# The second MLP of a two-layer block in two phases, with seven half products on each side

## The chip, the cores and the metric

The kernel runs on one NeuronCore of one Trainium2 chip. The metric is the device time of one execution in microseconds (us). Five engines work beside each other and meet through semaphores: TensorE (PE, matrix products), VectorE (DVE), ScalarE (ACT), GpSimd (POOL) and SyncE (SP, which issues most transfers). 16 DMA engines move data between DRAM and the core.

## The reference, cut to what matters

```python
for i in range(2):                      # layer 0: pooling mixer, layer 1: attention
    sh1, sc1, gt1, sh2, sc2, gt2 = ada_mods(c, w_ada[i], b_ada[i])
    ...                                 # the mixer of the layer
    m_lat = sq_relu_mlp(modulate(rms_norm(x, g_mlp_pre[i]), sh2, sc2), w_mlp_in[i], w_mlp_out[i])
    x = x + gt2 * rms_norm(m_lat, g_mlp_post[i])

def sq_relu_mlp(h, w_in, w_out):
    return jnp.square(jax.nn.relu(h @ w_in)) @ w_out
```

All of it is f32. The model width is 1024 and the hidden width of an MLP is 4096. The first MLP runs on 512 latent and 256 context tokens, the second on the 512 latent tokens alone. The second MLP therefore is a product of 512x1024 by 1024x4096 (the in-product), a squared relu, and a product of 512x4096 by 4096x1024 (the out-product).

## The kernel before, in words

**Precision.** Each f32 operand is split into a high part (a rounded copy, made by a cast on ACT) and a low part (the operand less its high part, a subtraction on DVE). A product of two f32 blocks is three matmuls: high by high, high by low, low by high. A "split" below means this pair of instructions.

**Groups and pairs.** The hidden width is cut into 16 groups of 256 columns; groups 2p and 2p+1 are pair p. Each group has 1 MB of in-weights and 1 MB of out-weights.

**The first MLP** (functions `mlp0`, `weights_sums`, `Seven`, `Halves`) has two phases. In the in-phase, groups 2 to 15 are done by `Seven`: the 2x2 block product of a group is formed from seven half products instead of eight, at the price of sums of weight blocks and sums of row blocks (`sums`, made once). The squares of a pair, and four sums of them, go to DRAM as seven row blocks (`lefts`, 384 KB each, written through POOL's queue). In the out-phase, `Halves` runs over the pairs in passes: pass by pass it takes one or two of the seven out-products, loads weights and row blocks again, splits them, and sums all seven pairs in the same PSUM banks, so that no product is added in SBUF until its last pair. Weights are loaded five steps ahead and prepared three steps ahead. An intermediate sum of weights (`halfway`) is written to DRAM in one pass and read back in a later one.

**The second MLP** (`mlp1`, lines 1210 to 1364) runs in one phase over seven pairs. Per pair it makes the in-products of two groups directly (`Inner`, L657: 48 matmuls of 128x512 for each group; the first two groups in column chunks of 256, 96 matmuls each), relus (L668) and squares (L1258) on ACT, and then the seven out-products of the pair before (`product`, L1267: two token tiles of six 128x512 matmuls each, 84 in all). Each half of a product is added to an accumulator in SBUF by DVE (L1271; the first pair is copied by ACT). Weight splits are at L1234 (out-weights and rows, with the sums at L1240) and at L199 and L202 (in-weights). Groups 14 and 15 are left for `finish`, which multiplies them by their out-weights directly, adds the accumulators and normalises.

**Buffers.** Working tiles of 128x1024 come from a ring of three (`work_tile`), raw weights of 1 MB from another ring of three (`rawp`). PSUM has eight banks: four in the pool `psB`, and either two double ones or four single ones in `psA` (`sum_banks`).

**What sets the order.** Up to the second MLP's first pair a scheduler places the instructions by its own estimate of their times; between `pin(True)` and `pin(False)` (in the first MLP) each engine's instructions stand in the order in which the program issues them. On every engine, and on every DMA issue queue, an instruction that waits holds up those behind it.

## Time and profile before

| | |
|---|---|
| time, median of 3 runs | 1119.65 us (1119.57 to 1119.93) |
| the profiled execution's own time | 1120.31 us |
| its span in the trace | 1118.5 us, so 1.8 us lie around the span |
| PE, DVE, ACT, POOL busy | 1099.2, 922.4, 620.2, 108.7 us |
| first MLP: in-phase, out-phase | up to 314 us, 314 to 514 us (49 steps of 18 matmuls) |
| second MLP | from about 783 us; the pairs to about 1089; the end to 1118 us |

The profile gives, for each engine, busy time and groups of equal instructions (line, engine, operation, output and inputs by the program's names, shape, count, busy time and mean time of one). Matmuls overlap, so the busy time of one (0.39 us for 128x512) is longer than the step from one start to the next. L95 is the line of a helper through which all instructions of the pinned parts go; they are told apart by the names of their tiles. `PEclk` is the granted clock of TensorE as a share of full speed.

### The profile page before, as it was taken

What the parts mean: (1) busy time and instruction counts of PE and PEld (TensorE: products, weight loads), DVE (VectorE), ACT (ScalarE), POOL (GpSimd) and SP (SyncE); (2) the same over time, 40 slices, a digit from 0 to 9 for tenths busy, and PEclk for the clock granted to TensorE, in tenths of its full rate; (3) what the DMA queues carried; (4) which work ended last, traced back from release to release, by engine and by line L of the source; (5) the groups of instructions that cost most, each with busy time, mean ns of one, the idle gap of its engine ahead of it and who ended that gap; (6) DMA issues with size and microseconds to landing.
All of it is one profiled execution on the core that took longest, in us unless ns stands there. A gap on an engine that the chain in (4) does not pass through costs nothing. (4 is left out here: it accounts for less than half of the span.)

```text
span 1118.5 us, 15827 instructions
## 1 busy us (share of the span) xinstructions
PE 1099.2 (98%) x6034; PEld 962.6 (86%) x6034; DVE 922.4 (82%) x1300; ACT 620.2 (55%) x1036; POOL 108.7 (10%) x176
## 2 busy tenths in 40 slices
PE   6999999999999999999999999999999999999997
PEld 6679999999988888887888899989988888888886
DVE  4888989999888889977776699885788888987876
ACT  6686566555564544443764478634674544543622
POOL 1240111111100000001242100002000000000001
PEclk9999999999999999999999999999999999999999
DMA  9984757767689989975211101172343333431212
GB/s 374 419 350 91 288 179 249 249 234 266 237 302 377 360 331 395 376 261 206 80 54 55 38 35 46 37 280 97 140 160 114 122 145 129 160 118 71 113 55 96
DMA packets 53371, 214.97 MB, mean 192 GB/s; under 512 B 7504, under 2 KB 10400, under 8 KB 38704
## 3 DMA queue, kind: packets, MB, share of 16 engines
q1 hardware_dynamic: 46688, 187.36, 45.3%
q0 software_dynamic: 6608, 26.61, 7.0%
q8 instruction: 47, 0.77, 0.3%
q14 instruction: 28, 0.23, 0.1%
HBM read 179.99 MB, written 33.96 MB: 191 GB/s over the span
## 5 line engine op out<-in xcount | busy, mean ns | idle before, releaser
L95 PE MATMUL pso<-ra,sums 128*128 128x512 f32 x594 | 135.8, 389 | 0.0
L95 PEld LDWEIGHTS pso<-ra,sums 128*128 128x128 f32 x594 | 111.5, 188 | 23.2
L657 PE MATMUL psin<-ra,rb 128*128 128x512 f32 (+1 forms) x310 | 87.5, 360 | 0.0
L1267 PE MATMUL pso<-units,pairs 128*128 128x512 f32 x336 | 82.8, 389 | 0.0
L657 PE MATMUL psin<-ra 128*128 128x512 f32 (+1 forms) x256 | 76.6, 376 | 0.0
L1267 PEld LDWEIGHTS pso<-units,pairs 128*128 128x128 f32 x336 | 63.1, 188 | 13.1
L1271 DVE TENSOR_TENSOR acc<-acc,pso 128x512 f32<-128x512 f32 x72 | 48.7, 680 | 22.4 <-PE pso L1267 22.4
L243 POOL TENSOR_SCALAR ms<-ss 128x1 f32<-128x1 f32 x15 | 10.1, 676 | 571.8 <-ACT junk L230 556.1
L95 PE MATMUL psin<-ra,units 128*128 128x384 f32 x340 | 63.4, 334 | 0.0
L657 PEld LDWEIGHTS psin<-ra,rb 128*128 128x128 f32 x310 | 55.5, 189 | 8.7
L95 PE MATMUL psin<-sums,units 128*128 128x384 f32 x308 | 62.4, 334 | 0.0
L95 DVE CUSTOM_DVE_ANT_0 waste<-raw,crow 128x1024 f32<-128x1024 f32 x50 | 61.1, 1222 | 1.3
L95 ACT CAST ra<-work 128x1024 fp32r<-128x1024 f32 x34 | 35.7, 1050 | 45.9 <-DVE work L95 42.4
L95 PEld LDWEIGHTS psin<-ra,units 128*128 128x128 f32 x340 | 59.3, 188 | 0.0
L95 PE MATMUL pso<-ra,rb 128*128 128x512 f32 x252 | 58.3, 389 | 0.0
L657 PE MATMUL psin<-rb,rb 128*128 128x512 f32 (+1 forms) x155 | 55.7, 360 | 0.1
L95 PEld LDWEIGHTS pso<-ra,rb 128*128 128x128 f32 x252 | 47.3, 188 | 9.8
L657 PEld LDWEIGHTS psin<-ra 128*128 128x128 f32 x256 | 47.1, 188 | 8.7
L95 PEld LDWEIGHTS psin<-sums,units 128*128 128x128 f32 x308 | 54.2, 188 | 0.1
L1418 PE MATMUL psq<-units,ra 128*128 128x512 f32 x216 | 52.2, 393 | 0.0
L95 DVE TENSOR_TENSOR ra<-work,ra 128x1024 fp32r<-128x1024 f32 x34 | 41.7, 1225 | 8.8 <-ACT ra L95 8.6
L657 PE MATMUL psin<-rb,ra 128*128 128x512 f32 (+1 forms) x128 | 48.1, 376 | 0.0
(333 smaller groups left out, 2673.5 us busy)
## 6 DMA issues: line engine op xcount, KB each, us to landing
raw<-in_w_ada SPq DMA_DIRECT2D x48, 1024.0 KB, 8.8
raw<-in_w_mlp_in SPq DMA_DIRECT2D x32, 1024.0 KB, 5.5
lefts<-acc POOLq DMA_DIRECT2D x48, 384.0 KB, 4.1
raw<-in_w_mlp_out SPq DMA_DIRECT2D x18, 1024.0 KB, 5.2
wide<-lefts SPq DMA_DIRECT2D x38, 384.0 KB, 7.3
wide<-in_w_mlp_out SPq DMA_DIRECT2D x21, 512.0 KB, 6.8
halfway<-work POOLq DMA_DIRECT2D x14, 512.0 KB, 7.8
raw<-in_w_mlp_out SPq DMA_DIRECT2D x14, 512.0 KB, 7.4
```

Source lines behind the costliest of these rows:

```text
L95: return lambda *args, **kw: self.tc.keep_in_program_order(f(*args, **kw))
L243: gp.tensor_scalar(out=ms[:, 0:1], in0=ss[:, parts - 1:parts], scalar1=rest, scalar2=EPS, op0=ALU.add, op1=ALU.add)
L657: te.matmul(ps[:, bank, o:o + ln], w[:, k, fs], rhs, start=start, stop=(k == KT - 1 and n == 2), skip_group_check=len(ks) < KT or self.paired)
L1267: te.matmul(ps, a, w, start=(m == 0), stop=(m == len(seq) - 1))
L1271: ve.tensor_tensor(out=M[n][:, t], in0=M[n][:, t], in1=ps, op=ALU.add)
L1418: te.matmul(ps, a[:, k, sl], w[:, k % 4, :], start=(k == 0 and n == 0), stop=(k == KT - 1 and n == 2))
```

## The change

The second MLP gets the two phases of the first.

In the ramp, groups 0 and 1 are done as before, and DVE and ACT make four sums of row blocks and their splits (`summed`) and the weights of group 2 (`weights`). Groups 2 to 15 then run through `Seven` with halves of 256 columns: seven products of twelve 128x256 matmuls a group, and two more "fresh" matmuls for each of the groups 2 and 3. Squares and their sums go to `lefts` in seven row blocks of 256 KB a pair. The dots of the last conditioning gate on DVE (sixteen of 512 columns, which stood beside the out-products) become eight of 1024 columns, two beside each of the groups 5, 7, 9 and 11.

The out-phase is a new class `Rows` with two passes: products 0, 4, 5 and 2 of all seven pairs, then products 6, 3 and 1, 49 steps of twelve 128x512 matmuls. A step's weights are a raw block (products 0, 2 and 1) or a difference that DVE makes first (4, 5, 6 and 3). For product 1 the low part is not made by DVE: ACT writes the negated high part and a DMA from POOL's queue adds the weights to it in SBUF. The results of a product are taken out of PSUM once, with its last pair. `xr`, `gate` and `junk` come back from DRAM in the second pass (`back`).

Three places show how the instructions move. DVE in the ramp, from the split of the second group on (`raw` is loaded weights, `work` a working tile, `units`, `ra` and `sums` hold split operands, `acc` rows). Before:

```order
L1234 TENSOR_TENSOR ra<-raw,ra 128x8x128
L1234 TENSOR_TENSOR ra<-raw,ra 128x1024
L1240 TENSOR_TENSOR work<-raw 128x1024
L1234 TENSOR_TENSOR ra<-work,ra 128x1024
L1234 TENSOR_TENSOR units<-raw,units 128x1024
L202 TENSOR_TENSOR rb<-raw,rb 128x2048
```

and now:

```order
L1443 TENSOR_TENSOR ra<-raw,ra 128x8x128
L1386 TENSOR_TENSOR work<-raw 128x1024
L1392 TENSOR_TENSOR work<-raw,work 128x512
L1411 TENSOR_TENSOR work<-acc 128x1024
L1393 TENSOR_TENSOR work<-raw,work 128x512
L1373 TENSOR_TENSOR units<-work,units 128x1024
L1414 TENSOR_TENSOR sums<-work,sums 128x1024
L1411 TENSOR_TENSOR work<-work,acc 128x1024
L1379 TENSOR_TENSOR units<-work,units 128x1024
```

After the split of group 1's weights DVE no longer splits out-weights: it forms sums of weights and of rows in working tiles (L1386, L1392, L1393, L1411) and their low parts (L1373, L1379, L1414). The second working tile that L1392 writes is the first tile of the ring of three come round again.

ACT at the same place now, from the cast of group 1's weights to the copy that stands after the first half product of group 2 (`psin` is PSUM):

```order
L1442 CAST ra<-raw 128x8x128
L668 ACTIVATE work<-psin 128x512 x2
L1439 ACTIVATE acc<-work 128x512 x2
L1372 CAST units<-work 128x1024
L1413 CAST sums<-work 128x1024
L1378 CAST units<-work 128x1024
L1413 CAST sums<-work 128x1024 x3
```

and right behind these rows come `L668` x2, `L1439` x2 for group 1 and then the copy within PSUM of group 2. The relus and squares of group 1 stand behind all casts of sums, where before relus, squares and casts alternated.

POOL's queue now, from the squares of the last pair to the second pass (before, POOL issues nothing in this MLP's pairs):

```order
L95 DMA lefts<-acc 128x2x256 x3
L95 DMA lefts<-acc 128x512 x4
L95 DMA halfway<-work 128x1024 x7
L95 DMA ra<-in_w_mlp_out 128x2x512
L95 DMA rb<-in_w_mlp_out 128x2x512
```

The seven writes of `halfway` belong to the first pass; the reads of weights into the operand slots in `ra` and `rb`, seven in all, are the accumulating transfers for product 1 in the second pass.

The diff, cut to its core:

```diff
@@ -794,7 +794,8 @@
 
         def run(self, behind):
             pool, tag = ((psB, "b"), (psA, "s"))[self.pool]
-            b, a, c, e = (pool.tile([P, 512], F32, tag=tag, name="psin")[:, 0:HN] for _ in range(4))
+            hn = self.to.shape[-1] // 2
+            b, a, c, e = (pool.tile([P, 512], F32, tag=tag, name="psin")[:, 0:hn] for _ in range(4))
...
+    class Rows:
+        PASSES = ((0, 4, 5, 2), (6, 3, 1))
+
...
+            self.rings = [ra[:, 2048 * n:2048 * n + 2048] for n in range(4)] + self.right[:2], \
+                [unit[0][:, 1024 * n:1024 * n + 1024] for n in range(4)] + self.left[:2]
+            self.hiddens, self.raws, self.rows, self.ops, self.banks, self.parts = hiddens, {}, {}, {}, {}, []
...
+        def load(self, j):
+            ps, p, n = self.todo[j]
+            at = lambda u, h: two(w_mlp_out[1, 2 * p + u])[:, :, 512 * h:512 * h + 512]
+            if n in (0, 5, 6, 3):
...
+            self.rows[j] = two(acc[:, c:c + 512])
+            sy.dma_start(self.rows[j], two(lefts[:, p, n, 0:LAT]))
+
+        def prepare(self, j):
+            ps, p, n = self.todo[j]
+            w = self.raws.pop((ps, p, {0: "11", 2: "22", 1: "21"}[n])) if n in (0, 2, 1) else two(work_tile())
+            sub = lambda a, b: ve.tensor_tensor(out=w, in0=a, in1=b, op=ALU.subtract)
+            if n == 0:
+                self.raws[ps, p, "11"] = w
+            if n == 4:
+                sub(self.raws.pop((ps, p, "12")), self.raws.pop((ps, p, "11")))
+                self.raws[ps, p, "t1"] = w
+            elif n == 5:
+                sub(self.raws[ps, p, "22"], self.raws.pop((ps, p, "t1")))
+                gp.dma_start(two(halfway[:, 1, p]), w)
+            elif n == 6:
+                sub(self.raws.pop((ps, p, "22")), self.raws.pop((ps, p, "12")))
+            elif n == 3:
+                sub(self.raws.pop((ps, p, "t2")), self.raws[ps, p, "21"])
+            r, l = (z[j] if j < 4 else g[(j - 4) % 6] for z, g in zip((self.right, self.left), self.rings))
+            wH, wL, aH, aL = two(r[:, 0:1024]), two(r[:, 1024:2048]), two(l[:, 0:512]), two(l[:, 512:1024])
+            a = self.rows.pop(j)
+            sc.copy(aH, a)
+            sc.copy(wH, w)
+            ve.tensor_tensor(out=aL, in0=a, in1=aH, op=ALU.subtract)
+            if n == 1:
+                sc.activation(wL, wH.bitcast(F32), AF.Copy, scale=-1.0)
+                gp.dma_start(wL, two(w_mlp_out[1, 2 * p + 1])[:, :, 0:512], accum_op=ALU.add)
+            else:
+                ve.tensor_tensor(out=wL, in0=w, in1=wH, op=ALU.subtract)
+            self.ops[j] = wH, wL, aH, aL
+
...
+        def multiply(self, j):
+            ps, p, n = self.todo[j]
+            wH, wL, aH, aL = self.ops.pop(j)
+            if p == 0:
+                pool, tag = ((psB, "b"), (psA, "s"))[n in (5, 2, 1)]
+                self.banks[n] = [pool.tile([P, 512], F32, tag=tag, name="pso") for _ in range(2)]
+            for q in range(2):
+                seq = [(a[:, f, P * q:P * q + P], w[:, f, :]) for f in range(2) for a, w in ((aH, wH), (aH, wL), (aL, wH))]
+                for m, (a, w) in enumerate(seq):
+                    te.matmul(self.banks[n][q], a, w, start=(p == 0 and m == 0),
+                              stop=(p == PAIRS - 1 and m == len(seq) - 1), skip_group_check=True)
+                if p == PAIRS - 1:
+                    self.take(n, q, self.banks[n][q])
...
+        def run(self, back):
+            far, last_ = 5, len(self.todo)
+            early = lambda j: j < last_ and self.todo[j][2] == 1
+            self.load(4)
+            self.prepare(2)
+            for j in range(last_):
+                ps, p, n = self.todo[j]
+                if j + far < last_:
+                    self.load(j + far)
+                self.multiply(j)
+                if j + 3 < last_ and not early(j + 3):
+                    self.prepare(j + 3)
+                if early(j + 4):
+                    self.prepare(j + 4)
+                if j in (3, 6):
+                    self.inner_rows(j // 3 - 1)
+                if j == 28:
+                    back()
+                if ps == 1 and 1 <= p <= 4 and n == 3:
...
+            def first_two():
+                w[0] = work_tile()
+                ve.tensor_tensor(out=words(w[0]), in0=rv[:, 1].rearrange("p (m k) n -> p m k n", m=2),
+                                 in1=rv[:, :, 0:4], op=ALU.subtract)
+
+            def last_two():
+                w[1] = work_tile()
+                t2, t4 = (k4(w[1][:, 512 * m:512 * m + 512]) for m in range(2))
+                ve.tensor_tensor(out=t2, in0=b22, in1=k4(w[0][:, 0:512]), op=ALU.subtract)
+                ve.tensor_tensor(out=t4, in0=b21, in1=t2, op=ALU.subtract)
...
+        def summed(n, a, b, op):
+            w = work_tile()
+            ve.tensor_tensor(out=w, in0=a, in1=b, op=op)
+            hi, lo = f[:, 2048 * n:2048 * n + 1024], f[:, 2048 * n + 1024:2048 * n + 2048]
+            sc.copy(hi, w)
+            ve.tensor_tensor(out=lo, in0=w, in1=hi, op=ALU.subtract)
             return w
...
-        def product(n, first_):
-            (aH, aL), (wH, wL) = X[operand[n]], W[n]
-            for t in range(2):
-                ps = psB.tile([P, 512], F32, tag="b", name="pso")
-                seq = [(a[:, f, t * P:t * P + P], w[:, f, :]) for f in range(2) for a, w in ((aH, wH), (aH, wL), (aL, wH))]
-                for m, (a, w) in enumerate(seq):
-                    te.matmul(ps, a, w, start=(m == 0), stop=(m == len(seq) - 1))
-                if first_:
-                    sc.copy(M[n][:, t], ps)
-                else:
-                    ve.tensor_tensor(out=M[n][:, t], in0=M[n][:, t], in1=ps, op=ALU.add)
...
+        def kept(p, n, z):
+            gp.dma_start(two(lefts[:, p, n, 0:LAT]), z)
...
+        def squared(inner, to):
+            for c in range(2):
+                for h in range(2):
+                    if (c, h) not in begun[inner]:
+                        inner.part(c, h)
+            for h in range(2):
+                sc.activation(to[:, h, :], inner.relu(h), AF.Square)
+
...
-        for p in range(NG // 2 - 1):
-            put(W[0], b11, p == 0)
-            put(W[1], both(1024, b22, b12, ALU.subtract, p == 0), p == 0)
-            put(W[2], b21, p == 0)
-            a11, a21 = squares(inner, 0)
...
+        raw = raw_load(w_mlp_in[1, 2])
+        steps, products = weights(2, raw)
+        squared(inner, first_hid)
+        for z in steps:
+            z()
+        w1 = summed(0, a21, a22, ALU.add)
+        w2 = summed(1, w1, a11, ALU.subtract)
+        summed(2, a11, a21, ALU.subtract)
+        summed(3, a12, w2, ALU.subtract)
+        squared(second, odd_hid)
+        raw = raw_load(w_mlp_in[1, 3])
+        sum_banks(True)
+        pin(True)
+        kept(0, 0, first_hid[:, :, 0:hn])
+        due = row_sums(0, first_hid, odd_hid)
+        chain = Rows(hids)
+        squares, late, dots1 = lambda: None, {g: j for j, g in enumerate((5, 7, 9, 11))}, {}
+        for g in range(2, NG):
+            seven = Seven(products, hids[g % 2], g % 2, g < 4)
+            behind = [[] for _ in range(8)]
+            if g < NG - 1:
+                steps, products = weights(g + 1, raw)
+                two_, four, bh, bl, ch, cl, th, tl, uh, ul = steps
+                for n, z in ((0, two_), (0, four), (3, bh), (3, ch), (3, bl), (4, th), (4, cl), (4, tl), (5, uh), (5, ul)):
+                    behind[n].append(z)
...
+            behind[1].append(rows_done)
+            if g in dots1:
+                j, dot = dots1.pop(g)
+                for b, n in enumerate((0, 2)):
+                    behind[n].append(lambda b=b, j=j, dot=dot: ada_dot(1, GT2, j, 1, dot, [accv[:, 3, :]], dot[:, D * b:D * b + D], b))
+            if g % 2 == 0 and g <= 2 * PAIRS:
+                behind[2].append(lambda: [due[n]() for n in range(3)])
+                behind[5].append(lambda: due[3]())
+            if g < NG - 2:
+                raw = raw_load(w_mlp_in[1, g + 2])
+            if g + 1 in late:
+                dots1[g + 1] = late[g + 1], raw_load(w_ada[1, GT2, late[g + 1]])
+            if g == NG - 1:
+                chain.begin()
+                behind[5].append(lambda: chain.prepare(0))
+                behind[7].append(lambda: chain.prepare(1))
+            squares = seven.run(lambda z: [f() for f in behind[z]])
+            if g == 2:
+                sy.dma_start(accv[:, 3, :], silu[0].partition_broadcast(P))
+        squares()
...
-        xr, gate, junk = residents(ctx)
-        for t in range(NL):
-            sy.dma_start(xr[:, t], spill[:, t])
-        finish(1, [(NG - 2 + q, last_[q].hid, wo_[q]) for q in range(2)], range(NL), last, ((5.1, gate_diag, 1, GT2, 0),))
+
+        def back():
+            nonlocal xr, gate, junk
+            xr, gate, junk = residents(ctx)
+            for t in range(NL):
+                sy.dma_start(xr[:, t], spill[:, t])
+
+        chain.run(back)
+        pin(False)
+        finish(1, chain.parts, range(NL), last, ((5.1, gate_diag, 1, GT2, 0),))
 
     alone = [(1, m, j) for m in (GT1, SC2, SH2) for j in range(4)]
```

More of the change, by code (lines that the diff above doesn't have):

```diff
@@ L1288, in mlp1 @@
-        wi = [None, None]
-        hi, lo = (ra[:, z:z + 2048] for z in (0, 2048))
-        hi, lo = (z.rearrange("p (k n) -> p k n", n=256) for z in (hi, lo))
-        put((hi[:, :, P:], lo[:, :, P:]), raw1[0][:, :, P:], True)
+        f = pool.tile([P, 8192], F32R, name="sums")
+        pool.tile([P, 520], F32, name="row")
+        hn = LAT // 2
+        first_hid, odd_hid, even_hid = (two(acc[:, z:z + 1024]) for z in (4096, 5120, 0))
+        hids = [even_hid, odd_hid]
+        mixed_rows = [two(acc[:, z:z + 512]) for z in range(1024, 3072, 512)]
@@ new lines, in kept, with row_sums, one @@
+        def kept(p, n, z):
+            gp.dma_start(two(lefts[:, p, n, 0:LAT]), z)
+        def row_sums(p, even, odd):
+            a11, a21, a12, a22 = (z[:, :, hn * h:hn * h + hn] for z in (even, odd) for h in range(2))
+            s1, s2, s3, s4 = mixed_rows
+            def one(n, d, a, b, op):
+                ve.tensor_tensor(out=d, in0=a, in1=b, op=op)
+                kept(p, n, d)
+            kept(p, 1, a12)
+            kept(p, 3, a22)
+            return [lambda: one(4, s1, a21, a22, ALU.add), lambda: one(5, s2, s1, a11, ALU.subtract),
+                    lambda: one(6, s3, a11, a21, ALU.subtract), lambda: one(2, s4, a12, s2, ALU.subtract)]
@@ new lines, in squared @@
+        def squared(inner, to):
[5 more added lines that the diff above has]
+                sc.activation(to[:, h, :], inner.relu(h), AF.Square)
+        hi, lo = (ra[:, z:z + 2048].rearrange("p (k n) -> p k n", n=256) for z in (0, 2048))
+        for z in (sc.copy(hi[:, :, P:], raw1[0][:, :, P:]),
+                  ve.tensor_tensor(out=lo[:, :, P:], in0=raw1[0][:, :, P:], in1=hi[:, :, P:], op=ALU.subtract)):
+            tc.keep_in_program_order(z)
```

215 lines of the change are left out of this document (98 added, 117 removed).

## The prediction

> **What bounds the kernel now.** I read the page's first part, the costliest groups, then the time line of PE and the table of windows.
>
> ```profile
> PE 1099.2 (98%) x6034; PEld 962.6 (86%) x6034; DVE 922.4 (82%) x1300; ACT 620.2 (55%) x1036; POOL 108.7 (10%) x176
> L1271 DVE TENSOR_TENSOR acc<-acc,pso 128x512 f32<-128x512 f32 x72 | 48.7, 680 | 22.4 <-PE pso L1267 22.4
> ```
>
> PE is busy all the time; DVE's adds of the out-products (L1271, 48.7 us) wait for PE, not PE for them. So the second MLP costs what its matmuls cost. On the time line of PE these rows bracket it (start, duration):
>
> ```profile
> 794.37 0.40 PE L657 MATMUL psin<-ra,rb 128*128 128x256 f32 x2
> 794.61 0.28 PE L657 MATMUL psin<-rb,rb 128*128 128x256 f32 x1
> 803.25 0.40 PE L657 MATMUL psin<-ra,rb 128*128 128x512 f32 x1
> 1088.88 1.52 PE L928 MATMUL pso<-ra,units 128*128 128x512 f32 x6
> ```
>
> From the first 512-column in-product (803.25) to `finish` (1088.88) are 285.63 us. In them stand 14 groups of 48 in-matmuls and 588 out-matmuls, 1260 in all: 226.7 ns each, without a gap. A 256-column matmul takes 120 ns from start to start (two in 0.24 us, at 794.37). In the windows (stretch, then PE, PEld, DVE, ACT and POOL busy, granted clock, DMA share, GB/s) the clock is full:
>
> ```profile
> 184.00:314.00 130.00, 130.00 (x752) 130.00 (x751) 123.93 (x178) 74.70 (x115) 17.76 (x29) 1.00 0.68 245
> 314.00:320.00 6.00, 6.00 (x30) 5.06 (x29) 3.95 (x5) 5.05 (x7) 0.54 (x1) 1.00 1.00 378
> 430.00:480.00 50.00, 50.00 (x222) 41.39 (x221) 45.62 (x47) 24.46 (x28) 0.00 (x0) 1.00 0.97 366
> 844.00:966.00 122.00, 122.00 (x540) 101.02 (x539) 100.54 (x132) 57.88 (x71) 0.00 (x0) 1.00 0.36 130
> ```
>
> The last row is the second MLP: DVE 82% busy, DMA at a third. The first three are the first MLP, which has the new form already: its in-phase with DVE at 95%, its turn to the out-phase, and its third pass with DMA at 97%, all with PE full. They are the measure for what the change asks for.
>
> **The change part by part.**
>
> *PE's work.* A group's in-product goes from 48 x 0.2267 = 10.88 us to 84 x 0.120 = 10.08 us: -0.80 us, over 14 groups **-11.2 us**. Four fresh matmuls add 0.48. The out-products keep their 588 matmuls. The adds that go (L1271) were hidden, so they bring nothing. The Trainium skill ("TensorE: Matmul & The Clock Gate", section "Back-to-back issue gap") gives about 131 ns a matmul of 512 columns and 81 ns of 128 in a stream with weight loads; by an estimate between them a 256-column matmul takes some 98 ns, and 84 of these against 48 of 131 would lose 1.9 us a group. The rows at 226.7 and 120 ns contradict it here, so it gets no chance.
>
> *The ramp.* This is where I expect the first stall. Rows for the durations (DVE, then ACT):
>
> ```profile
> 790.67 2.35 DVE L1234 TENSOR_TENSOR ra<-raw,ra 128x1024 fp32r<-128x1024 f32 x2
> 802.25 0.69 DVE L1234 TENSOR_TENSOR pairs<-work,pairs 128x512 fp32r<-128x512 f32 x1
> 789.55 2.01 ACT L1234 CAST ra<-raw 128x1024 fp32r<-128x1024 f32 x2
> 798.54 1.08 ACT L668 ACTIVATE work<-psin 128x512 f32<-128x512 f32 x2
> 799.51 1.15 ACT L1258 ACTIVATE hid<-work 128x512 f32<-128x512 f32 x2
> ```
>
> A 1024-wide DVE operation steps by about 1.14 us and a 512-wide one by 0.61 in a row. In the new order of PE group 0's last matmul stands 70 before the end of the 256-column stretch, so it ends at 803.25 - 70 x 0.12 = 794.85. Its two relus and one square (1.08 + 0.6) give 796.6. Only then does the ring of three working tiles free the one that L1392 writes: DVE waits from about 793. From 796.6 it has L1392, L1411, L1393 (0.61 + 1.14 + 0.61) and seven 1024-wide operations (8.0) to the last row sum: 807.0. ACT casts that sum (1.05): 808.05. Behind the cast, in ACT's order, stand group 1's relus and squares (2.2): 810.3, and behind these the copy within PSUM of group 2 (a 128x256 one, estimated 0.35): 810.65. PE's third half product of group 2 needs that copy, and PE would come to it at 803.25 + 0.24 + 2 x 1.44 = 806.4. **+4.3 us.** The same wait in the first MLP, in the table of waits:
>
> ```profile
> PE psin L95 <- ACT psin L95: 0.7, 1, 0.7
> ```
>
> So the bounds are 0.7 and, if DVE's lag of some 1.2 us behind it costs group 3 too, 5.5. I take 4.3.
>
> *The in-phase* asks of DVE, at these steps, about 7.1 us a group and 2.4 a pair for the row sums: 16.6 of 20.16 us, with the gate's dots in groups 4 to 11 19.1 of 20.16 (95%). The first MLP did 95% without a gap: 0, at most 0.1 us a group if the shorter steps (1.44 us a product instead of 2.08) leave less slack: +1.
>
> *The turn to the out-phase.* Steps 0 to 2 are prepared only after group 15's fifth product. A step with a difference takes a chain of DVE 1.14, ACT 1.05, DVE 1.14: 3.3 us, against a PE step of 12 x 0.2267 = 2.72 us. Following DVE and ACT in order I get PE waits of 0.15, 0.95 and 0.7 us for the first three steps and 0.85 after the rows of the last groups are split (step 10): **+2.65.** In the first MLP the same turn shows none (314 to 320, PE full), but its steps are 4.08 us long. Bounds 0 and two chains, 6.6. After that DVE has about 10.2 of 10.88 us a pair in the first pass, and transfers 23 MiB in 76 us (316 GB/s), below what the rows show: 0.
>
> *The second pass.* No row shows the accumulating transfer. The nearest are the third pass of the first MLP, on the time line of SP's queue:
>
> ```profile
> 444.81 0.33 SPq L95 DMA_DIRECT2D wide<-lefts  x1
> 451.92 0.33 SPq L95 DMA_DIRECT2D wide<-lefts  x1
> 459.03 0.33 SPq L95 DMA_DIRECT2D wide<-lefts  x1
> ```
>
> and the page's table of issues (KB each, median us from issue to landing), POOL's writes:
>
> ```profile
> lefts<-acc POOLq DMA_DIRECT2D x48, 384.0 KB, 4.1
> ...
> halfway<-work POOLq DMA_DIRECT2D x14, 512.0 KB, 7.8
> ```
>
> There one pair's 2.75 MiB come every 7.11 us: 405 GB/s, with DMA full. So DMA gives about 405. The new second pass wants per pair 2 MiB of weights, 0.75 of rows and 0.5 of accumulation, 3.25 MiB in a PE time of 3 x 2.72 = 8.16 us: 418 GB/s, and 2 MiB of last weights beside. What must move while PE does the 18 steps from the pass's start to its last load is 20.4 MB (five pairs' loads and a row block 14.25 MiB, seven accumulations 3.5, last weights 2): 50.4 us at 405 against 49.0. That is +1.4 if an accumulation counts once. It reads its destination too: counted twice, 24.1 MB take 59.5 us, **+10.5.** Apart from bandwidth, the first one can be issued only behind the take-out of product 5 and a cast, about 3.4 us into the pass, and is wanted 5.7 us in: at a landing time of 4.1 us PE waits 1.8, at 7.8 us 5.5. Bounds 1.4 and 12; I take **+3.5**, between the two landings and nearer to one transfer than to two, since SBUF's side is written anyway.
>
> `finish` is the same matmuls as before: 0.
>
> *Sum* against the profiled execution: 1120.31 - 11.2 + 0.48 + 4.3 + 2.65 + 3.5 = 1120.0. The median lies 0.66 below the profiled time: 1119.4. Waits that I have not found only add; I forecast **1119.8 us**, no change: the gain of 11 us is given back in three places.
>
> **The rivals.**
>
> *A, covered:* the turn and the second pass hide as in the first MLP, and the ramp costs between 0.7 and 4.3 us: 1119.65 - 10.72 + 0.7 (or 4.3) = 1109.6 to 1113.2, or with one of the two stalls half there up to 1117. For it speak the three windows of the first MLP with PE full; against it that all PE steps are a third shorter here with equal work on weights.
>
> *B, the accumulation fills the second pass* (the other side): seven transfers that occupy the DMA engines twice. 1119.65 - 10.72 + 4.3 + 2.65 + 10.5 to 12 = 1126.4 to 1127.9. It decides from the point where the stall of the pass exceeds 3.8 us, which is (49.0 + 3.8) x 405 = 21.4 MB, an accumulation counted 1.27 times. For it: DMA at 97% in the window 430 to 480, and more wanted per us here. Against: the prefetch of two pairs, and POOL's 384 KB in 4.1 us. A sentence of the Trainium skill speaks for B ("DMA: Bandwidth & Descriptors", section "Rules for kernel authors"): an accumulate reads its destination and writes it later; no trace here shows what that costs.
>
> *C, the in-phase falls behind:* with steps of 1.44 us PE waits at a copy or an add of each group, 0.4 us x 14 = 5.6: 1119.8 + 5.6 = 1125.4. For it: DVE at 95% in groups 4 to 11; against: the first MLP at the same share.
>
> That the change doesn't do what it says I give nothing: the order of PE's instructions has the 84 short matmuls a group.
>
> **How the numbers follow.** About 0.2% (2.2 us) can be told from no change: faster is below 1117.4, slower above 1121.9. The forecast has 0.40, over its own range 1116 to 1123: of that 0.28 same, 0.06 faster, 0.06 slower. A has 0.32, all faster. B has 0.21 and C 0.07, all slower. Faster 0.38, same 0.28, slower 0.34. Since both sides hold much, the range reaches into A and through B: 1111 to 1128.5.
>
> **What would show it.** 84 in-matmuls a group at 120 ns, and PE's wait of 4 us for an ACT copy within PSUM near 806, confirm the first two steps. PE waits for split weights in the first three out-steps (0.7 to 1 us each) confirm the third. In the second pass, PE's waits for the accumulating transfer: one of 2 to 5 us in its first pair is the forecast; one in every pair with DMA at its full share is B; none is A. PE idle in every group is C. The forecast is wrong if PE's idle time from 803 to `finish` is below 8 us or above 13 us.

## The result, and the profile after

The changed kernel takes **1144.04 us** (1143.49 to 1144.91) against 1119.61 (1119.54 to 1119.93) in the same comparison: a ratio of 1.0218 [1.0201, 1.0236], 24.4 us slower. The prediction of 1119.8 and its range up to 1128.5 are both missed.

The first part of the page of the changed kernel:

```profile
PE 1098.7 (96%) x6542; PEld 982.1 (86%) x6542; DVE 941.5 (82%) x1314; ACT 664.7 (58%) x1151; POOL 150.0 (13%) x239
```

PE's busy time is that of before (1098.7 against 1099.2) although it has 11 us less to do: part of its work ran at a lower clock. From its table of windows, the in-phase, the first and the second pass of the out-phase (stretch, then PE, PEld, DVE, ACT and POOL busy, granted clock, DMA share, GB/s):

```profile
803.00:950.00 147.00, 143.04 (x1181) 142.84 (x1180) 129.64 (x171) 98.88 (x183) 29.84 (x48) 0.99 0.62 217
950.00:1030.00 80.00, 77.78 (x342) 63.02 (x341) 70.97 (x76) 49.14 (x67) 3.73 (x7) 1.00 0.85 301
1030.00:1112.00 82.00, 64.93 (x255) 50.75 (x254) 56.30 (x63) 41.92 (x50) 7.63 (x7) 0.90 0.87 275
```

PE's idle time is 3.96 us in the first window, 2.2 in the second and 17.1 in the third, 23.2 in all, where the prediction named 13 as its limit. The table of waits names what ended them (us in total, times, longest; the table is that of the whole program, rows of other parts are left out, and 0.7 us of the second row lie in the first MLP):

```profile
PE pso L95 <- DMA ra<-in_w_mlp_out: 14.1, 4, 7.8
...
PE psin L95 <- ACT psin L95: 4.7, 2, 4.0
PE pso L95 <- ACT ra L95: 1.6, 2, 1.4
PE pso L95 <- DVE ra L95: 1.5, 2, 0.8
...
PE pso L95 <- DMA rb<-in_w_mlp_out: 0.8, 1, 0.8
```

On the time line of PE (start, duration; in brackets the idle time before and what ended it):

```profile
810.71 2.93 PE L95 MATMUL psin<-sums,units 128*128 128x256 f32 x12 [3.96 <-ACT psin L95]
1034.89 0.50 PE L95 MATMUL pso<-ra,rb 128*128 128x512 f32 x1 [1.41 <-ACT ra L95]
1036.15 4.42 PE L95 MATMUL pso<-ra,rb 128*128 128x512 f32 x12 [0.76 <-DVE ra L95]
1048.38 7.57 PE L95 MATMUL pso<-ra,rb 128*128 128x512 f32 x23 [7.80 <-DMA ra<-in_w_mlp_out]
1090.14 7.11 PE L95 MATMUL pso<-ra,rb 128*128 128x512 f32 x23 [3.36 <-DMA ra<-in_w_mlp_out]
1112.24 5.60 PE L929 MATMUL pso<-units,ra 128*128 128x512 f32 x24
```

The wait in the ramp and the wait for the accumulating transfer (`ra` or `rb<-in_w_mlp_out`) are there. But 12 matmuls behind the first took 2.93 us, and 23 behind the 7.80 us wait took 7.57: 0.24 and 0.33 us each instead of 0.12 and 0.2267. The windows of 2 us at these two places (and at 1036, behind the waits of 1.41 and 0.76 us) show why:

```profile
808.00:810.00 2.00, 0.00 (x0) 0.00 (x0) 1.97 (x3) 2.00 (x5) 0.00 (x0) 1.00 0.00 0
810.00:812.00 2.00, 1.29 (x6) 1.29 (x7) 1.86 (x3) 0.96 (x3) 1.16 (x2) 0.62 0.00 0
812.00:814.00 2.00, 2.00 (x11) 2.00 (x11) 1.97 (x4) 0.32 (x2) 0.89 (x2) 0.52 0.76 264
814.00:816.00 2.00, 2.00 (x19) 2.00 (x18) 1.30 (x2) 2.00 (x5) 1.08 (x2) 1.00 0.65 242
1036.00:1038.00 2.00, 1.85 (x4) 1.49 (x5) 2.00 (x5) 1.87 (x3) 0.11 (x1) 0.50 0.47 160
1050.00:1052.00 2.00, 2.00 (x7) 1.52 (x6) 1.56 (x2) 1.66 (x2) 0.00 (x0) 0.50 1.05 393
```

Behind the wait in the ramp the granted clock (the third number from the end) is 0.52 to 0.62 for some 3.4 us, and 11 matmuls go where 19 went before. Not every wait is followed by this: behind those of 1.64, 0.83 and 1.25 us in the second pass the windows show 1.00. `finish` starts at 1112.24 instead of 1088.88: 23.4 us, nearly the whole loss. Against the steps of PE, the in-phase with the ramp's wait, from group 2's first matmul at 803.48 to 950.68, lost 5.6 us (147.2 for 1180 x 0.120 = 141.6), the first pass from 950.68 to 1030.60 lost 3.8 (79.9 for 28 x 12 x 0.2267 = 76.2), and the second from 1030.60 to 1112.24 lost 24.5 (81.6 for 57.1). Less the 10.7 us of saved work that is the 23.4, to within 0.2 us.

DMA queues in the window 1020 to 1110 (packets, MB, share of 16 engines), and issues there (KB each, us to landing):

```profile
q1 hardware_dynamic: 9876, 21.42, 65.2%
q0 software_dynamic: 2048, 4.19, 24.0%
...
ra<-in_w_mlp_out POOLq DMA_DIRECT2D x4, 512.0 KB, 9.7
```

A megabyte on POOL's queue (the second row: seven accumulations and one plain write of `halfway`) takes 5.73% of the window's engine time, a plain one on SP's queue (the first row) 3.04%: 1.88 times as much.

### The profile page after: what moved, and what is told of

Same layout as the page of the kernel before. It is cut to its first block, busy times and chain, and to the rows that moved or that the text cites. A ratio compares the mean times of both kernels' runs of the same rounds, so it can differ in the third digit from the quotient of the medians.

```text
span 1142.1 us, 17327 instructions
## 1 busy us (share of the span) xinstructions
PE 1098.7 (96%) x6542; PEld 982.1 (86%) x6542; DVE 941.5 (82%) x1314; ACT 664.7 (58%) x1151; POOL 150.0 (13%) x239
## 4 chain that ended last, share of the span: by engine, by line
PE 22%; issue 16%; DVE 4%; DMA 4%; POOL 2%; ACT 2%; POOLq 0%; DVEq 0%; SPq 0%; ACTq 0%
PE psin L95 12%; PE pso L95 5%; DMA work<-in_w_mlp_out 3%; PE psq L1564 2%; PE pso L929 2%; DVE work L95 1%; POOL rs L1573 1%; POOL rs L245 1%; ACT ra L95 1%; PE psin L657 1%; DMA ra<-in_w_mlp_out 1%; ACT rb L95 0%; ACT units L95 0%; DVE units L95 0%; DVE work L1411 0%
## 5 line engine op out<-in xcount | busy, mean ns | idle before, releaser
L95 PE MATMUL pso<-ra,rb 128*128 128x512 f32 x624 | 151.2, 400 | 17.1 <-DMA ra<-in_w_mlp_out 14.1
L95 PEld LDWEIGHTS pso<-ra,rb 128*128 128x128 f32 x624 | 120.3, 194 | 45.7 <-DMA ra<-in_w_mlp_out 15.7
L95 PEld LDWEIGHTS pso<-ra,sums 128*128 128x128 f32 x594 | 111.5, 188 | 23.2
L95 PE MATMUL psin<-sums,units 128*128 128x256 f32 (+1 forms) x644 | 106.5, 310 | 4.0 <-ACT psin L95 4.0
L95 POOL DMA_DIRECT2D lefts<-acc x97 | 60.6, 628 | 302.5 <-ACT work L95 185.8
L95 PE MATMUL psin<-ra,units 128*128 128x384 f32 (+1 forms) x510 | 97.5, 317 | 0.0
L95 DVE TENSOR_TENSOR work<-raw 128x1024 f32<-128x1024 f32 x56 | 68.2, 1217 | 0.7 <-DMA raw<-in_w_mlp_out 0.6
L95 DVE CUSTOM_DVE_ANT_0 waste<-raw,crow 128x1024 f32<-128x1024 f32 x50 | 61.1, 1223 | 1.3
L95 PE MATMUL psin<-sums,ra 128*128 128x256 f32 (+1 forms) x420 | 58.3, 293 | 0.0
L95 PEld LDWEIGHTS psin<-sums,ra 128*128 128x128 f32 x420 | 56.0, 191 | 0.0
L95 PE MATMUL psin<-ra 128*128 128x256 f32 (+1 forms) x254 | 49.6, 300 | 0.0
L95 PE MATMUL pso<-rb 128*128 128x512 f32 x192 | 46.0, 392 | 1.7 <-DMA rb<-in_w_mlp_out 0.8
```

The lines of the kernel that those rows point to most:

```text
L95: return lambda *args, **kw: self.tc.keep_in_program_order(f(*args, **kw))
```

## The experiments

All times are medians; the kernel before had 1119.9 to 1120.6 in these comparisons. "The relieved version" is described in part 3. None of them beats the kernel before with the whole computation.

**1. Second pass: is it the transfer, or the queues behind it?** My first theory was the accumulating transfer, the rival ACT's and DVE's queues, blocked by the last weights, which are loaded into working tiles. One run makes the low part of product 1 on DVE, one loads the last weights a pair earlier, one replaces the accumulation by a plain copy.

```diff
-            if n == 1:
-                sc.activation(wL, wH.bitcast(F32), AF.Copy, scale=-1.0)
-                gp.dma_start(wL, two(w_mlp_out[1, 2 * p + 1])[:, :, 0:512], accum_op=ALU.add)
-            else:
-                ve.tensor_tensor(out=wL, in0=w, in1=wH, op=ALU.subtract)
+            ve.tensor_tensor(out=wL, in0=w, in1=wH, op=ALU.subtract)
```

> The low weights of product 1 are made by DVE like all others; the seven accumulating transfers are gone, nothing else changes. Theory 1 (the accumulating transfer, late and moved twice, is what PE waits for in the second pass): all five waits of the second pass on transfers (7.80, 1.64, 0.83, 3.36, 1.25 us) and the low clock behind them go, 1144.0 to about 1120 to 1122 us. Theory 2 (ACT and DVE stand still at the cast of the last groups' weights until a load issued in the same step lands, and later steps' operands come late): the first and the last wait go, waits of 1 to 3 us stay in the pairs with last weights, about 1127 to 1131. If DVE becomes the bound by its additional 1.14 us a pair (8.7 of 8.16 us in four pairs): 1124 to 1126 with PE waiting for DVE.

Measured: 1134.12 us, 9.9 less than the change (net of the work that DVE takes on), but still 1.0130 [1.0115, 1.0145] of before, above all three ranges: the third branch by what PE waits for, with its size missed. Its table of waits has no DMA left in the out-phase:

```profile
PE pso L95 <- DVE ra L95: 5.9, 9, 0.8
PE pso L95 <- ACT ra L95: 2.3, 4, 1.4
PE pso L95 <- DVE rb L95: 1.9, 3, 0.8
```

PE now waits for DVE's low parts. The second pass takes 71.2 us, 14.1 more than PE's steps.

```diff
-            w = work_tile()
-            sy.dma_start(w, w_mlp_out[1, NG - 2 + q][:, D * f:D * f + D])
+            w = xr[:, 4 + f]
...
+        def last_load(self, q, f):
+            sy.dma_start(xr[:, 4 + f], w_mlp_out[1, NG - 2 + q][:, D * f:D * f + D])
```

> Same transfers as the changed kernel, but each of the four loads of last weights is issued one pair (three steps) before its split, into a buffer of its own. Theory 2 (blocked ACT and DVE): the waits 1.64, 0.83 and 3.36 us go with their low clock, about 1134 to 1137 us, the first wait of 7.8 us stays. Theory 1 (bytes and double accumulation): the bytes are the same, so the time stays, 1142 to 1145.

Measured: 1143.97 us, 1.0219 [1.0203, 1.0234]: no gain, the longest wait for the accumulation is 8.6 us. The blocked queues are refuted as its cause.

```diff
-                gp.dma_start(wL, two(w_mlp_out[1, 2 * p + 1])[:, :, 0:512], accum_op=ALU.add)
+                gp.dma_start(wL, two(w_mlp_out[1, 2 * p + 1])[:, :, 0:512])
```

> The seven transfers for product 1 copy the weights into the slot instead of adding them to it (the low part of product 1 is then wrong; place, size, queue and waits are the same). Theory 1a (an addition moves its bytes twice): the share of the DMA engines per MB on POOL's queue falls from 1.9 times that of SP's queue to about 1, landing falls from 9.7 to about 7 us, PE's first wait from 7.8 to about 5 and the later ones from 7.1 in sum to below 3: 1144.0 to about 1134 to 1137 us. Theory 1b (being one more transfer, issued late, is what counts, whatever it does): 1142 to 1145.

Measured: 1137.68 us, 1.0157 [1.0141, 1.0172], 0.7 above the range of theory 1a and far below that of 1b. So the addition itself costs 6.4 us. PE's first wait for a transfer in the second pass falls from 7.80 to 5.57 us. POOL's queue (the second row) in the same window:

```profile
q1 hardware_dynamic: 9985, 21.63, 66.2%
q0 software_dynamic: 2048, 4.19, 15.0%
...
ra<-in_w_mlp_out POOLq DMA_DIRECT2D x4, 512.0 KB, 8.1
```

15.0% against 24.0% for the same bytes, the write of `halfway` among them: with additions the queue takes 1.6 times the engine time that it takes with copies, and an addition lands 1.6 us later.

**2. The ramp: the ring of working tiles, and the clock.**

```diff
-                sc.activation(to[:, h, :], inner.relu(h), AF.Square)
+                for b0, nb, ln, t0 in inner.pieces:
+                    sc.activation(to[:, h, t0:t0 + nb * ln].rearrange("p (b n) -> p b n", n=ln), inner.ps[h][:, b0:b0 + nb, 0:ln], AF.Relu)
+                sc.activation(to[:, h, :], to[:, h, :], AF.Square)
```

> Groups 0 and 1 write their relu to the place of the square and square it there, so that no working tile is held for them. If the ring of three tiles is the cause of the ramp's wait, DVE starts its sums some 3.7 us earlier, PE's wait of 3.96 us falls below 1 us: 1144.0 to about 1140 if only the wait goes, 1138 to 1139 if the half clock of the following 12 matmuls goes with it. If the order of ACT behind the sums is the cause alone: 1143 to 1144.

Measured: 1140.90 us, 1.0190 [1.0173, 1.0207]: 3.1 less, not the whole. The wait at 806 is gone, so the ring of working tiles was its cause, but the scheduler moved DVE's first sum of weights ahead of a normalisation that PE needs; that wait (`psx`, ended by `acc`) grew from 0.9 to 2.8 us, with the half clock behind it. With the same edit and that sum kept behind group 1's split:

```diff
-                ve.tensor_tensor(out=words(w[0]), in0=rv[:, 1].rearrange("p (m k) n -> p m k n", m=2),
+                z = ve.tensor_tensor(out=words(w[0]), in0=rv[:, 1].rearrange("p (m k) n -> p m k n", m=2),
...
+                if g == 2:
+                    tc.keep_in_program_order(z)
```

> As the run without working tiles for the first relus, and the first weight sum of group 2 is held behind the split of group 1, so that the sums don't move ahead of the normalisation as they did there. If that move is what gave part of the gain back (PE's wait for the normalisation grew from 0.9 to 2.8 us, with half clock behind it), both waits are now below 1 us: 1144.0 minus 3.96 minus 1.7 gives 1138 to 1139; the run before it had 1140.9. If the ring's wait only moves on within the ramp: 1141 to 1144.

Measured: 1137.33 us, 1.0152 [1.0138, 1.0166]: 6.7 us less than the change. In the traces the stretch from group 2's first matmul to the out-phase goes from 147.2 to 142.2 us, 5.0 less, where the wait fell from 3.96 to 0.31; the other 1.7 us lie behind the in-phase. Of the 5.0, 1.35 are more than the wait and should be the clock. So one run fills the wait with 30 matmuls of 128x256 whose result is overwritten:

```diff
+            for m in range(self.warm):
+                te.matmul(c, wH[0], aH[0], start=True, stop=True, skip_group_check=True)
```

> 30 additional matmuls of 128x256 into a bank that is overwritten behind them stand in group 2 where PE waits for ACT's copy (3.96 us), so that PE works through the wait. The wait itself stays as long. If the low granted clock behind the wait (0.5 for about 3.4 us) comes from PE standing still, it goes and 1144.0 falls to about 1142.3. If it does not: 1144 or slightly more.

Measured: 1141.39 us, 1.0189 [1.0175, 1.0203]: with more work it is 2.6 us faster. The same stretch takes 145.8 us for 147.2, so 1.4 of the 2.6 us are here; the rest lies behind the in-phase. Its windows at the same place:

```profile
808.00:810.00 2.00, 2.00 (x19) 2.00 (x19) 2.00 (x2) 2.00 (x4) 0.00 (x0) 1.00 0.00 0
810.00:812.00 2.00, 1.63 (x14) 1.43 (x13) 1.86 (x3) 1.35 (x4) 0.78 (x2) 1.00 0.00 0
812.00:814.00 2.00, 2.00 (x19) 2.00 (x18) 1.93 (x4) 1.17 (x2) 0.89 (x2) 1.00 0.65 225
```

The clock stays at 1.00 and 19 matmuls go where 11 went: the half clock comes from PE standing still, and 1.4 us is its price here. The Trainium skill says so as a rule ("TensorE: Matmul & The Clock Gate", section "Why this matters for your kernels"): no gaps over about 3 us between bursts, or the clock falls to 4/8. The 3.96 us gap agrees. In these runs single waits of 2.53 and 2.81 us (first ramp run) already had a clock of 0.53 to 0.62 behind them, and one of 2.45 us (plain copy) had 1.00. In the changed kernel two gaps of 1.41 and 0.76 us, half a microsecond apart, stand beside a clock of 0.50 at 1036 to 1038; the first ramp run has the same two gaps at a clock of 1.00, so two short gaps do not always bring it.

**3. All three, and a relieved version.** Edits 1 (DVE's low part, early last weights) and the first ramp edit together:

> All three edits together (low weights on DVE, last weights loaded a pair earlier, no working tiles for the first relus). If these waits and the clock behind them are the whole loss, what stays is the turn (2.1 us) and up to 3 us of DVE in the second pass: 1111 to 1115 us, faster than before. If the transfers of the second pass as such are too many (2.75 MiB a pair and the last weights), 1118 to 1122.

Measured: 1130.09 us, 1.0089 [1.0074, 1.0104], above both ranges. A window late in its second pass:

```profile
1080.00:1090.00 10.00, 8.84 (x37) 6.62 (x38) 8.82 (x10) 5.56 (x7) 0.00 (x0) 1.00 0.50 189
```

DVE is 88% busy with DMA at half, and I took its chain per step (difference, ACT's cast, low part) for what PE follows. The relieved version therefore also splits the last weights beside group 15, pins the ramp's sum, prepares steps 0 to 2 beside group 15, makes both differences of a pair together and takes results out behind the next step's preparation.

```diff
+                self.ahead[p] = two(work_tile())
+                sub(self.raws.pop((ps, p, "t2")), self.raws[ps, p, "21"], self.ahead[p])
...
+                behind[2 * q + h].append(lambda q=q, h=h: chain.last_weights(q, h, ends[q]))
...
+                behind[6].append(lambda: chain.prepare(1))
+                behind[7].append(lambda: chain.prepare(2))
```

> The three edits, and DVE's chain in the out-phase relieved: the last groups' weights are split during group 15, both differences of a pair in the second pass are made one behind the other, results are taken from PSUM after the next step's operands, steps 0 to 2 are prepared during group 15. If DVE's time per pair (9.97 us measured for 8.16 us of PE with the three edits) is what is left: the second pass loses 1 to 3 us, the turn below 1, the ramp below 1: 1119.6 - 10.7 + 2 to 5 = 1111 to 1114 us, faster than before. If transfers bound the second pass now (2.75 MiB a pair at 405 GB/s take 7.1 us): also 1111 to 1114. If ACT or the loads' buffers hold it: 1117 to 1122.

Measured: 1122.25 us, 1.0014 [1.0006, 1.0023]: another 7.8 us (its edits were not separated), but 8 to 11 us above what I expected, and nearest to the branch in which ACT or the loads' buffers hold it. The profiled execution took 1120.72; in it `finish` starts at 1089.79 and the second pass takes 62.1 us for 57.1. Two further orders bring nothing that can be told:

```diff
+                if p:
+                    self.ahead[p] = two(work_tile())
+                    sub(self.raws[ps, p, "22"], w, self.ahead[p])
...
-                add(c22, c21, c12)
+                gp.tensor_tensor(out=c22, in0=c21, in1=c12, op=ALU.add)
```

> The relieved kernel, with both differences of a pair made one behind the other in the first pass too, the last groups' weights and steps 0 and 1 prepared earlier in group 15, and one of two additions at the take-out of product 5 on POOL. If DVE's order and time are what is left (2.7 us in the turn, 1.9 in the rest of the first pass, 5.0 in the second): losses of 1.5, 0.3 and 3, 1122.2 - 4.8 = 1117 to 1118, faster than before. If these come from transfers that land late: 1120 to 1123.

Measured: 1122.30 us, 1.0024 [1.0015, 1.0034], in the range for transfers that land late; ACT's casts beside group 15 hold up a copy in PSUM (1.0 us), and PE's waits for DVE stay.

```diff
-                for q in range(2) if p == PAIRS - 1 else ():
-                    self.take(n, q, self.banks[n][q])
+                for m in [j - 1] + [j] * (j == last_ - 1):
+                    for q in range(2) if m >= 0 and self.todo[m][1] == PAIRS - 1 else ():
+                        self.take(self.todo[m][2], q, self.banks[self.todo[m][2]][q])
```

> The relieved version with the second of these edits alone: the take-outs stand one step later on VectorE's queue. Theory 1 (the take-outs hold VectorE and by it the ring of raw tiles and the next loads): 1119.5 to 1121.5 us. Theory 2 (the chain difference, cast, low part is too long for a step of 2.72 us wherever the take-outs stand): 1122 us, no change.

Measured: 1121.18 us, 1.0010 [1.0001, 1.0019]: within the uncertainty of the relieved version.

**4. What holds the relieved version 13 us above PE's work?** DVE's time in the out-phase, or loads, which keep DMA 75 to 89% busy there. The runs that follow leave out part of the work or of the loads, so their outputs are not those of the reference:

```diff
-            ve.tensor_tensor(out=aL, in0=a, in1=aH, op=ALU.subtract)
+            if ps == 0:
+                ve.tensor_tensor(out=aL, in0=a, in1=aH, op=ALU.subtract)
```

> The relieved kernel, with the low parts of the row blocks left out in the second pass (21 subtractions of 0.61 us on DVE; what is multiplied there is left from the first pass, all matmuls, casts and transfers stay). Its second pass took 62.1 us for 57.1 us of PE. If DVE's time holds the second pass, it falls to 57 to 58.5 us: 1122.2 (median; 1120.8 in the profiled run) minus 3.5 to 5 gives 1117 to 1118.5. If transfers or ACT hold it: 1121 to 1122.

Measured: 1120.46 us, 1.0003 [0.9995, 1.0012]: 1.8 us less, between the two ranges and with an interval that meets that of the relieved version.

```diff
-            ve.tensor_tensor(out=aL, in0=a, in1=aH, op=ALU.subtract)
-            ve.tensor_tensor(out=wL, in0=w, in1=wH, op=ALU.subtract)
-            self.ops[j] = wH, wL, aH, aL
+            self.ops[j] = wH, wH, aH, aH
```

> The relieved version (1122.25 us) without the low halves of weights and rows in the whole out-phase: TensorE reads the high halves in their place, so the out-products are those of rounded operands. About 40 of VectorE's 54 us in the second pass go, loads stay. Theory 1, VectorE's time holds the out-phase: the turn's 2.7, the first pass's 1.9 and the second pass's 5.0 us go to about 1 in all: 1112 to 1114 us. Theory 2, loads hold it (302 to 344 GB/s were had from 1030 to 1070 us, 2.75 MiB a pair in 8.16 us want 353): the second pass keeps its 4 to 5 us and the turn its casts: 1116 to 1119 us.

Measured: 1111.58 us, 0.9919 [0.9905, 0.9934]: 10.7 us less, slightly below the range of theory 1.

```diff
-                sub(self.raws.pop((ps, p, "12")), self.raws.pop((ps, p, "11")))
+                w = self.raws.pop((ps, p, "12"))
...
-                sub(self.raws[ps, p, "22"], self.raws.pop((ps, p, "t1")))
+                w = self.raws[ps, p, "22"]
...
-                sub(self.raws.pop((ps, p, "22")), self.raws.pop((ps, p, "12")))
+                w = self.raws.pop((ps, p, "22"))
```

> The relieved version without the differences of weight blocks: a step casts a block as loaded, so products 3 to 6 have other weights. The chain of a step is one VectorE operation of 1.22 us shorter, VectorE has 15 of 54 us less in the second pass, loads stay. Theory 1, VectorE's time or chain: 1112 to 1117 us, with no PE wait for VectorE's low halves in the second pass. Theory 2, loads: 1117 to 1121 us.

Measured: 1117.52 us, 0.9974 [0.9963, 0.9985]: 4.7 us less: half a microsecond above theory 1's range and at the lower end of theory 2's. Four PE waits for DVE are left in the second pass (2.9 us), which theory 1 excluded.

```diff
-            sy.dma_start(self.rows[j], two(lefts[:, p, n, 0:LAT]))
+            if j < 20:
+                sy.dma_start(self.rows[j], two(lefts[:, p, n, 0:LAT]))
...
-                    sy.dma_start(b, at(0, 1))
-                    self.raws[ps, p, "22"], self.raws[ps, p, "12"] = a, b
+                    self.raws[ps, p, "22"], self.raws[ps, p, "12"] = a, a
```

> The relieved version with 1.25 of the 2.75 MiB a pair not loaded in the second pass (the row blocks from the first pass's last two pairs on, and block 12 of the weights, for which block 22 is taken; these products have wrong operands). VectorE and ScalarE do all they did. Theory 1, VectorE's time and chain hold the second pass: 1121 to 1122.5 us. Theory 2, loads that come late hold it: its 5.0 us go to about 1, 1117.5 to 1119 us.

Measured: 1120.15 us, 0.9994 [0.9985, 1.0003]: 2.1 us less, at the edge of what can be told and between the two theories. The windows of the two passes, first of the relieved version:

```profile
950.00:1030.00 80.00, 77.67 (x336) 62.41 (x336) 71.16 (x75) 50.05 (x68) 3.73 (x7) 1.00 0.89 311
1030.00:1090.00 60.00, 56.71 (x244) 45.25 (x243) 54.83 (x63) 27.16 (x36) 0.00 (x0) 1.00 0.75 264
```

then without low halves:

```profile
950.00:1030.00 80.00, 80.00 (x355) 66.24 (x354) 26.97 (x25) 53.09 (x72) 3.20 (x6) 1.00 0.96 355
1030.00:1090.00 60.00, 60.00 (x267) 49.64 (x266) 22.88 (x28) 24.88 (x36) 0.87 (x2) 1.00 0.55 204
```

and with fewer loads:

```profile
950.00:1030.00 80.00, 77.70 (x337) 62.36 (x335) 71.20 (x75) 50.32 (x69) 3.74 (x7) 1.00 0.75 268
1030.00:1090.00 60.00, 57.76 (x245) 46.78 (x244) 54.84 (x64) 26.80 (x36) 0.00 (x0) 0.97 0.40 133
```

Without low halves, with DVE's work more than halved, PE has no gap at all, though DMA is busier in the first pass than in the relieved version (0.96 against 0.89). So it is by way of DVE's low halves that PE is held up. But whether DVE's time or late loads hold these up is not decided by the totals. The traces of the five runs give, by pass (us; PE alone needs 76.2 and 57.1):

| run | first pass | second pass | DVE busy, 1030 to 1090 |
|---|---|---|---|
| relieved | 80.7 | 62.1 | 54.8 |
| no low halves of rows in the second pass | 80.7 | 63.0 | 44.8 |
| no low halves | 76.2 | 57.1 | 22.9 |
| no differences | 76.5 | 62.1 | 37.4 |
| fewer loads in the second pass | 80.8 | 61.8 | 54.8 |

In the first pass, leaving out DVE's differences is enough: there DVE's part of the chain holds PE. In the second pass no single relief shortens the trace by more than 2 us. (Behind short waits, 1.7 us of the 63.0 and 1.5 of the 61.8 are matmuls at half clock, of which the relieved trace shows none.) The run without differences shows why. Its second pass (window, then waits in 1030 to 1090: us in total, times, longest):

```profile
1030.00:1090.00 60.00, 56.98 (x244) 45.21 (x243) 37.42 (x46) 23.61 (x32) 0.00 (x0) 1.00 0.67 231
...
DVE rb L95 <- ACT rb L95: 19.5, 5, 4.8
ACT rb L95 <- DMA acc<-lefts: 19.3, 4, 5.1
...
SPq L95 <- DVE ra L95: 19.6, 5, 5.6
```

With DVE at 37.4 of 60 us PE still waits for DVE; but DVE waits for ACT's casts, these wait for row blocks, and SP issues loads late because it waits for DVE to be done with their buffers (this edit keeps a raw block until its low half is made). In the relieved version two of PE's five waits in the pass (0.30 and 0.76 us) follow waits of DVE for raw weights (2.8 us), and they are gone with fewer loads; the other three (0.32, 0.67 and 1.24 us, at its start) stand while DVE works without a gap from 1030 to 1051. So in the second pass DVE's time and the loads that wait for its buffers hold PE together; which share is whose stays open. The groups of DVE in the second pass of the relieved version (1030 to 1108; busy, mean ns) give its demand:

```profile
L95 DVE TENSOR_TENSOR work<-raw 128x1024 f32<-128x1024 f32 x12 | 14.3, 1220 | 2.8 <-DMA raw<-in_w_mlp_out 2.8
L95 DVE TENSOR_TENSOR rb<-acc,rb 128x512 fp32r<-128x512 f32 x19 | 13.0, 686 | 0.4 <-ACT rb L95 0.3
L95 DVE TENSOR_TENSOR ra<-work,ra 128x1024 fp32r<-128x1024 f32 x9 | 11.0, 1223 | 0.7 <-ACT ra L95 0.5
```

A pair needs two differences, three low halves of weights and three of rows: 5 x 1.22 + 3 x 0.69 = 8.2 us by the mean times, or 7.5 by the steps of such operations in a row (1.14 and 0.61). PE's three steps take 8.16. DVE has nearly as much to do as PE, and every take-out (0.68) and every wait of DVE comes on top.

**5. Half of the row work to GpSimd?** The edit of the take-outs, and the low half of the rows on GpSimd:

```diff
-            ve.tensor_tensor(out=aL, in0=a, in1=aH, op=ALU.subtract)
+            gp.tensor_tensor(out=aL, in0=a, in1=aH, op=ALU.subtract)
```

> The relieved version (1122.25 us median) with two edits. In the second pass of the out-products the low half of a row block (row minus its high half) is formed by GpSimd instead of VectorE, and an output column's two take-outs from PSUM stand on VectorE's queue one step later, so that they no longer hold the difference of the next step back while they wait for TensorE's last matmul. Theory 1: VectorE's time per pair and its take-out waits hold the pass. Leaving the row lows out altogether was worth 1.8 us; moving them keeps that, and the later take-outs give back the 0.7 to 0.9 us waits of the pass's first steps: 1116 to 1119 us. Theory 2: row loads that arrive late and the casts behind them hold it, or GpSimd's slower operation comes on the path: 1120.5 to 1124 us, with PE waits for GpSimd in the table of waits.

The edit moved the low halves of both passes. Measured: 1146.37 us, 1.0232 [1.0218, 1.0246]: 25 us worse than with the late take-outs alone, far outside both ranges. The page's table of the costliest groups has POOL's subtractions:

```profile
L95 POOL TENSOR_TENSOR rb<-acc,rb 128x512 fp32r<-128x512 f32 x47 | 78.9, 1699 | 38.0 <-ACT rb L95 37.9
```

and the groups of DVE from 1030 to 1108 have the low halves of differences, to be compared with the last row of DVE's groups in part 4:

```profile
L95 DVE TENSOR_TENSOR ra<-work,ra 128x1024 fp32r<-128x1024 f32 x13 | 25.2, 1959 | 7.0 <-ACT ra L95 6.9
```

PE never waits for POOL; it waits for DVE, whose operation on two SBUF operands went from 1223 to 1959 ns beside POOL's. The Trainium skill has this ("GPSIMD Engine Reference", section "Specifications"): GpSimd's way to SBUF is shared with VectorE and contends where that reads two SBUF inputs. The trace agrees, at 1.6 times; what POOL took off DVE (0.69 us a step) came back as longer low halves of weights (0.74 us each for this row).

## Why the prediction was wrong, step by step

**PE's work, -11.2 + 0.48: right.** Without low halves PE runs both passes without a gap and `finish` starts at 1080.17, 8.7 us earlier than before, with what remains of the ramp in it; its two passes take 133.3 us, 588 x 0.2267.

**The ramp, +4.3: mechanism right, size too small.** The wait for the copy behind the casts was 3.96 us at 806.75, through the ring of working tiles, as worked out: PE went on at 810.71, where the prediction had 810.65. The term measured 5.6 us in the trace, just above its bound of 5.5, since about 1.4 us of half clock stand behind the wait (run with the wait filled). The prediction had no price for a clock that falls.

**The in-phase, 0 (+1): right.** Apart from the ramp PE has no gap up to 950, with DVE at 129.6 of 147 us. Rival C did not happen.

**The turn, +2.65: mechanism right, size somewhat small.** There are 2.1 us of waits for split rows and weights in the first three steps and at step 10 behind the row splits; with what PE lost without a visible wait, 3.8 us to the end of the first pass, within the bounds of 0 and 6.6.

**The second pass, +3.5 (bounds 1.4 and 12): this is the step that failed.** It measured 24.5 us. In the trace these are 14.9 us of PE's waits for the accumulating transfer, 2.2 of waits for ACT and DVE at the pass's start, and 7.4 by which the matmuls took longer, at a mean granted clock of 0.90.

First, the transfer, which the prediction priced "nearer to one transfer than to two". Leaving out its addition brings 6.4 us, taking it away 9.9 net of DVE's new work. Rival B had this mechanism and put it at 10.5 to 12, and the engine time of 1.88 lies past its point of 1.27 (so the sentence of the Trainium skill that spoke for B, "DMA: Bandwidth & Descriptors", section "Rules for kernel authors", agrees). The first wait was 7.80 us, not 1.8 to 5.5. The transfer was issued 7.3 us into the pass instead of 3.4, and PE came to it 10.0 in instead of 5.7, so these two shifts nearly cancel; the landing took 9.7 us (median), not 4.1 to 7.8. A plain copy in its place landed in 8.1, near the upper bound, with a wait of 5.57: what the rows of plain writes could not show is the addition.

Second, the half clock behind the longer waits: 23 matmuls took 7.4 us behind the wait of 7.80 and 6.95 behind that of 3.36, for 5.2. The prediction had no price for it here either.

Third, what stands behind the transfer. The prediction summed DVE's time for the first pass (10.2 of 10.88 us) and never for the second. Without the transfer, product 1's low half is DVE's, which then has 7.5 to 8.2 of PE's 8.16 us a pair, with the last weights beside, and the pass still took 71.2 us for 57.1. In the changed kernel itself little of this shows as a wait for DVE (0.76 us). It was no term, no bound and no rival, and it is why taking the transfer away gave 9.9 us and not 24. How the 7.8 us of the relieved version divide among the last weights moved away, the order of the differences and the turn stays open, and so does what share of its last 5.0 us in this pass is DVE's and what the loads'.

A slip in the sum: the parts that the prediction lists for the transfers (14.25, 3.5 and 2 MiB) add to 20.7 MB, not 20.4. Five pairs and a row block are 14.0 MiB, which gives the 20.4; by the list as written the +1.4 would be +2.1. It changes nothing above.

**Finish, 0: right.** It takes 29.9 us from its first matmul to the end of the span, and 29.6 before.

**Rival A** failed by its main ground, the first MLP's windows with PE full. There a step is 4.08 us for the same work on weights; here it is 2.72. The prediction named this and still gave A a third.

## What to carry to other kernels

A scheme that saves matmuls by sums of operands moves work from PE to the engines that prepare operands. Before taking it to a smaller tile, divide: time of an operand's preparation on the busiest engine by PE's time for the step, for every pass by itself. The quotient warns but does not decide: the first MLP's in-phase kept PE full with DVE 95% busy, and the second pass without differences had waits with DVE at 62%, since loads and buffers belong to the same chain. And price a wait of PE of 2.5 us or more with the half clock behind it, here 1.4 to 2.2 us.

## What the runs showed of the hardware that I had not expected

- A wait of 3.96 us was followed by about 3.4 us at a granted clock of 0.52 to 0.62. Filling the wait with matmuls whose result is overwritten kept the clock at 1.00 and shortened that stretch by 1.4 us. Waits of 2.53 us and more had a low clock behind them, one of 2.45 us had not; two short ones close together (1.41 and 0.76 us) had it in the changed kernel and not in the first ramp run.
- POOL's queue with transfers that add into SBUF took 1.88 times the engine time per MB of the plain loads beside it, and 1.6 times that of plain copies of the same bytes on the same queue (24.0% against 15.0%).
- GpSimd subtractions beside it slowed DVE's two-operand subtraction from 1223 to 1959 ns.
